# Stick-breaking attention: sums over later key blocks on TensorE instead of GpSimd, float32 scores instead of stacked float32r scores

## The chip, the cores and the metric

The kernel runs on one core of one Trainium2 chip. The metric is the device time of one execution in microseconds (us). The kernel before took 813.81, 815.24 and 815.90 us in three runs; their median, 815.24 us, is "the time before". A core has five engines, named here as in the profile: PE (TensorE, the matrix unit, with PEld for its weight loads), DVE (VectorE), ACT (ScalarE), POOL (GpSimd) and SP (SyncE, which issues DMAs). Matrix products are written to PSUM, which has banks of 512 float32 values per partition; everything else lies in SBUF. Each engine works through its own queue in order.

## The reference, cut to what matters

One decoder layer for 512 tokens of width 1024 in float32: a norm, one wide input projection, two attention branches, a gated merge, an output projection, a SwiGLU feed-forward part and a last norm. The change concerns the first branch, stick-breaking attention with 8 heads of 64 features:

```python
z = einsum('bhqd,bkhd->bhqk', q_blk, k) * scale
causal = kpos[None, :] < tpos[:, None]
log_keep = where(causal, log_sigmoid(-z), 0.0)
log_after = cumsum(log_keep, axis=3, reverse=True) - log_keep
a = where(causal, exp(log_sigmoid(z) + log_after), 0.0)
out = einsum('bhqk,bkhd->bqhd', a, v)
```

With softplus(z) = -log_sigmoid(-z), the log weight of key j for query q is z[j,q] minus the sum of softplus(z[j',q]) over all keys j' from j up to the query. The sum runs over the key's own block of 128 keys and over all later blocks.

## The kernel before, in words

Activations lie feature-major ([feature, token]). Each large product is made of three float32r products, with both operands split into a high and a low part: ACT casts the high part, DVE subtracts to get the low part (`split_to`, lines 103 to 105; weights in `split_chunk`, lines 78 to 85). SP loads the weight chunks of 512 KB. A planner (the tile framework, with a simulated time line) puts the instructions of each engine in a fixed order at build time; instructions whose operands the planner expects in time are interleaved, so the products of later projections stand between those of the attention.

The order of the program is: input and norm; for each of four pairs of heads n the projections of q and k (`proj_feature`, lines 233 to 243; the values v for all heads once, `proj_token`) and then `sb_pair`; the projections of the dilated branch and its attention (`dil_pair`, two pairs); the gates; the merge; the output projection; the feed-forward part, which fills the time from about 400 us on.

PSUM's eight banks are split into 2 for projections ("proj"), 5 for attention ("att") and 1 for outputs ("o") (line 26). SBUF tiles come from pools with a fixed number of buffers (line 27): NT = 10 for the float32 tiles t and r, NR = 9 for the high and low parts h and l, NS = 10 for the stacked operands.

`sb_pair` (lines 297 to 393) handles two heads. Keys are in four blocks a = 0 to 3 of 128; block a has scores for the queries from a x 128 on, thus 512, 384, 256 and 128 columns. Tile names end with the pair's number and with x, y or z: x is a head's blocks 1 and 3 together in one bank (384 + 128 columns), y is block 2 of both heads in one bank (2 x 256), z is a head's block 0 (512). So a pair has five banks: two x, one y, two z.

1. Stacking (lines 302 to 310): for each head ks holds the high and the low part of its 64 key rows above each other on 128 partitions, qa the high part of the queries twice, qb the low part twice. ACT makes three casts, DVE three subtractions per head, on 64 rows x 512.
2. Scores (lines 312 to 325): for blocks 0 to 2 two float32r products over 128 rows (ks with qa, ks with qb); for block 3 one float32 product over the head's 64 rows. A bf16 product of an identity and a mask adds a large negative value where a key isn't before its query.
3. Softplus (`breaks`, lines 327 to 337): ACT takes absolute value, exponent and logarithm, DVE adds max(z, 0), `split_to` makes h and l, and two float32r products with the triangular matrix `tri` (minus one) subtract the block's own running sums in PSUM.
4. Sums for the other blocks (`total`, lines 339 to 342): POOL sums each t tile over the partitions and leaves the sum on all of them (r), three times per pair. POOL adds the sums of several blocks up (lines 364 and 367).
5. Exponents: `later` (lines 346 to 348) subtracts r from PSUM on DVE in the columns that have later key blocks, then ACT takes the exponent; `plain` (lines 350 to 352) takes the exponent directly from PSUM elsewhere.
6. The output product (line 385): float32, the weights of both heads in the two halves of the array's columns, blocks 0 to 3, then a split of the result.

The next pair's score products need the banks that the exponents and subtractions of the pair before give free. In `dil_pair` the score products (lines 398 and 402) are float32 over the 64 rows of one head, 128 columns each.

Of the kernel before, what the change touches and what calls it, by code (L numbers as in the profile page):

```python
# [10 lines left out]
F32 = mybir.dt.float32  # L11
# [15 lines left out]
RAW, NT, NR, NQ, NS = 3, 10, 9, 16, 10  # L27
# [3 lines left out]
def trunk_kernel(ctx, tc, xT, gains, w_in, w_up, w_o, w_f, w_d, bias, out):  # L31
    """Activations are kept feature-major ([feature, token]); the weights are the
    stationary operands. Every float32 operand of the large products is split into
    two float32r parts (hi + lo, exact) and three of the four part products are
    accumulated; the fourth lies below float32's rounding.  The norms' row factors
    commute with the products and are applied where the products leave PSUM."""
# [11 lines left out]
    # products on zeros while the first loads are under way: the PE clock is up when they arrive  # L48
# [127 lines left out]
    V.tensor_copy(tri, tri0)  # L176
    mask0 = ap_.tile([P, S], F32, tag="t", name="mask0", bufs=NT)[:, :2 * P].rearrange("p (a b) -> p a b", a=2)
# [5 lines left out]
    # token blocks of a group: 128 neighbours, or every fourth token (dilation 4; for dilation 16  # L183
    # each such block holds four of the sixteen residues)
# [60 lines left out]
    def proj_token(name, kind, wide):  # L245
        # token-major: the tokens' blocks are stationary, the weights move
        v = ap_.tile([P, 4, wide], F32, tag=name, name=name)
        nk = 1024 // wide
        if wide == 512:
            banks = [bank("att", f"pv{name}{c}") for c in range(4)]  # L250
            order = [(j, c) for j in range(KD // nk) for c in range(4)]
            w = {}
        else:
            w = {0: next_weights(), 1: next_weights(1)}
            order = [(j, c) for c in range(4) for j in range(KD // nk)]
            banks = {}
        for j, c in order:
            if j not in w:
                w[j] = next_weights()
            if c not in banks if wide != 512 else False:  # L260
                banks[c] = bank("proj", f"pv{name}{c}")
            ps = banks[c][:, :wide]
            whi, wlo = w[j]
            for i in range(nk):
                k = j * nk + i
                cs = slice(i * wide, (i + 1) * wide)
                mm3(ps, blk(xh[k], kind, c), blk(xl[k], kind, c), whi[:, cs], wlo[:, cs], k == 0, k == KD - 1)
            if j == KD // nk - 1:
# [26 lines left out]
    # log weight of key j for query q: z[j,q] - sum_{j'>=j} softplus(z[j',q]); key blocks 1 and 3  # L295
    # of a head share a bank, and so do the two heads' blocks 2
    def sb_pair(n, q, k, v, hb):
        hs = [slice(0, 64), slice(64, 128)]

        # both parts of a head's keys fill the 128 rows, so two products carry all four part products  # L300
        ks, qa, qb = [], [], []
        for h in range(2):
            ks.append(stack(f"ks{n}{h}"))
            qa.append(stack(f"qa{n}{h}"))
            qb.append(stack(f"qb{n}{h}"))
            A.copy(ks[h][hs[0]], k[hs[h]])
            V.tensor_tensor(out=ks[h][hs[1]], in0=k[hs[h]], in1=ks[h][hs[0]].bitcast(F32), op=ALU.subtract)
            for r in hs:
                A.copy(qa[h][r], q[hs[h]])
                V.tensor_tensor(out=qb[h][r], in0=q[hs[h]], in1=qa[h][r].bitcast(F32), op=ALU.subtract)  # L310

        def score(ps, o, h, a, start):
            ps = ps[:, o:o + S - a * P]
            if a < 3:
                T.matmul(ps, ks[h][:, a * P:(a + 1) * P], qa[h][:, a * P:], start=start, stop=False, skip_group_check=True)
                T.matmul(ps, ks[h][:, a * P:(a + 1) * P], qb[h][:, a * P:], start=False, stop=False, skip_group_check=True)
            else:
                T.matmul(ps, k[hs[h], a * P:], q[hs[h], a * P:], start=start, stop=False, skip_group_check=True)

        def scores(name, parts, masked):  # L320
            ps = bank("att", f"z{n}{name}")
            for i, (h, a, o) in enumerate(parts):
                score(ps, o, h, a, i == 0)
            T.matmul(ps.rearrange("p (a b) -> p a b", b=P)[:, masked, :], idb, mask[:, :len(parts)], start=False, stop=False, skip_group_check=True)
            return ps

        def breaks(name, ps):
            t = tt(f"t{n}{name}")
# [4 lines left out]
            hi, lo = rt(f"h{n}{name}"), rt(f"l{n}{name}")  # L333
            split_to(hi, lo, t)
            T.matmul(ps, tri, hi, start=False, stop=False, skip_group_check=True)
            T.matmul(ps, tri, lo, start=False, stop=True, skip_group_check=True)
            return ps, t

        def total(name, t):
            r = tt(f"r{n}{name}")  # L340
            G.partition_all_reduce(r, t, P, bass_isa.ReduceOp.add)
            return r

        # A key block's softplus sums count for all the earlier key blocks of the same queries:
        # t = exp(ps - r) in the columns that have later key blocks, exp(ps) in the others
        def later(ps, t, cs, r):
            V.tensor_tensor(out=t[:, cs], in0=ps[:, cs], in1=r, op=ALU.subtract)
            A.activation(t[:, cs], t[:, cs], AF.Exp)

        def plain(ps, t, cols):  # L350
            v = lambda y: y.rearrange("p (a b) -> p a b", b=P)[:, cols, :]
            A.activation(v(t), v(ps), AF.Exp)

        z13 = [scores(f"x{h}", [(h, 1, 0), (h, 3, 384)], slice(0, 4, 3)) for h in range(2)]
        z2 = scores("y", [(0, 2, 0), (1, 2, 256)], slice(0, 4, 2))
        b13 = [breaks(f"x{h}", z13[h]) for h in range(2)]
        b2 = breaks("y", z2)
        r13 = [total(f"x{h}", b13[h][1]) for h in range(2)]
        r2 = total("y", b2[1])
        plain(*b2, slice(0, 4, 2))  # L360
        for h in range(2):
            o = 256 * h
            later(*b2, slice(o + 128, o + 256), r13[h][:, 384:512])
            G.tensor_tensor(out=r2[:, o + 128:o + 256], in0=r2[:, o + 128:o + 256], in1=r13[h][:, 384:512], op=ALU.add)
            plain(*b13[h], slice(0, 4, 3))
            later(*b13[h], slice(128, 384), r2[:, o:o + 256])
            G.tensor_tensor(out=r13[h][:, 128:384], in0=r13[h][:, 128:384], in1=r2[:, o:o + 256], op=ALU.add)
        z0 = [scores(f"z{h}", [(h, 0, 0)], slice(0, 1)) for h in range(2)]
        b0 = [breaks(f"z{h}", z0[h]) for h in range(2)]
        for h in range(2):  # L370
            plain(*b0[h], slice(0, 1))
            later(*b0[h], slice(128, 512), r13[h][:, 0:384])
        po = bank("o", f"o{n}")
        for a in range(4):
            for h in range(2):
                if a == 0:
                    m = b0[h][1]
                elif a == 1:
                    m = b13[h][1][:, 0:384]
                elif a == 2:  # L380
                    m = b2[1][:, 256 * h:256 * h + 256]
                else:
                    m = b13[h][1][:, 384:512]
                c = (hb + h) * 64
                T.matmul(po[hs[h], a * P:], v[:, a, c:c + 64], m, start=a == 0, stop=a == 3, skip_group_check=True)
        split_out(f"s{n}", po)

# [204 lines left out]
    for half in range(2):  # L592
# [5 lines left out]
        if half:  # L598
            # the PE keeps its clock while the norm's row factors are worked out
# [92 lines left out]
```

## Time and profile before

| | |
|---|---|
| median of three timed runs | 815.24 us (813.81 to 815.90) |
| profiled execution, first to last instruction | 814.5 us |
| PE busy | 795.1 us, 98% of the span |
| DVE, ACT, POOL busy | 398.7, 307.7, 123.2 us |
| 51 to 154 us (most of stick-breaking): PE, DVE, ACT, POOL busy of 103.0 | 94.39, 79.13, 75.56, 49.72 |
| PE's mean granted clock, whole span | 0.973 |

All times in the profile are of that one execution; 814.5 us is its span, and what the timed runs have beside it is the 0.7 us by which their median is longer. A row of a timeline has the start, the length, the engine, the line, the operation, the tiles (out<-in), shapes, and in brackets the idle time before it and who ended it. The length of a PE row includes the time in which the next product is already under way, so the cost of a product is read from the distance of two starts. A float32 product leaves two records, a float32r product one. L99, L100 and L101 are the three part products of `mm3`.

### The profile page before, as it was taken

The page shows a single profiled execution, that of the slowest core. Times are in us where ns is not written, and L with a number is a line of the kernel's source. Part 1 is how long each engine was busy: PE and PEld are TensorE (multiplying, and loading weights), DVE is VectorE, ACT ScalarE, POOL GpSimd, SP SyncE. Part 2 cuts the span into 40 slices and gives each one's busy share as a digit, 9 for nine tenths or more (in the row PEclk, how much of TensorE's full clock was granted, in tenths as well). Part 3 has the DMA queues.
Part 4 walks back from the last instruction along what each step waited for, and adds up shares of the span by engine and source line. Part 5 has one row for each costly group of instructions (what it writes and reads, how often), then busy time and mean ns, then how long its engine had stood idle before and what let it go on. Part 6 is the DMA issues. An engine that isn't in the chain of part 4 may idle for free.

```text
span 814.5 us, 9164 instructions
## 1 busy us (share of the span) xinstructions
PE 795.1 (98%) x3635; PEld 649.5 (80%) x3635; DVE 398.7 (49%) x490; ACT 307.7 (38%) x453; POOL 123.2 (15%) x94
## 2 busy tenths in 40 slices
PE   8999988999999999999999999999999999999995
PEld 5877656878997787788888888888888888888885
DVE  6379885543245375438653544444444444322312
ACT  7277865622113335223343432233323322332321
POOL 3424534500003103100232000000000000010012
PEclk9999998999978899999999999999999999999998
DMA  7321111052311103123543223222332333333302
GB/s 234 128 79 52 52 53 52 27 170 89 103 52 52 52 26 105 49 75 109 171 142 102 81 100 104 103 85 97 103 100 83 103 97 97 94 94 97 97 20 103
DMA packets 23786, 74.00 MB, mean 91 GB/s; under 512 B 2608, under 2 KB 5696, under 8 KB 23616
## 3 DMA queue, kind: packets, MB, share of 16 engines
q1 hardware_dynamic: 22928, 70.26, 26.6%
q0 software_dynamic: 816, 3.16, 1.1%
q8 instruction: 28, 0.46, 0.2%
q14 instruction: 14, 0.11, 0.0%
HBM read 71.32 MB, written 2.10 MB: 90 GB/s over the span
## 4 chain that ended last, share of the span: by engine, by line
PE 59%; DVE 0%; ACT 0%; POOL 0%; DVEq 0%; issue 0%; POOLq 0%
PE pd L100 5%; PE pd L101 5%; PE pd L99 5%; PE pu L101 5%; PE pg L101 5%; PE pg L99 5%; PE pu L99 5%; PE pu L100 5%; PE pg L100 5%; PE po L100 2%; PE po L99 2%; PE po L101 2%; PE us L101 1%; PE us L100 1%; PE us L99 1%; PE pjgd L100 1%
## 5 line engine op out<-in xcount | busy, mean ns | idle before, releaser
L83 ACT CAST whi<-raw 128x1024 fp32r<-128x1024 f32 (+1 forms) x128 | 131.2, 1025 | 383.6 <-PE pu L100 77.8
L84 DVE TENSOR_TENSOR wlo<-raw,whi 128x1024 fp32r<-128x1024 f32 (+1 forms) x128 | 159.5, 1247 | 101.8 <-ACT whi L83 101.7
L99 PE MATMUL pd<-hh,whi 128*128 128x512 f32 (+1 forms) x198 | 72.6, 367 | 0.0
L100 PE MATMUL pd<-hl,whi 128*128 128x512 f32 (+1 forms) x198 | 72.4, 366 | 0.0
L101 PE MATMUL pd<-hh,wlo 128*128 128x512 f32 (+1 forms) x198 | 72.3, 365 | 0.0
L101 PE MATMUL pg<-uh,wlo 128*128 128x512 f32 x176 | 68.9, 391 | 0.0
L101 PE MATMUL pu<-uh,wlo 128*128 128x512 f32 x176 | 68.6, 390 | 0.0
L100 PE MATMUL pu<-ul,whi 128*128 128x512 f32 x176 | 68.5, 389 | 0.0
L100 PE MATMUL pg<-ul,whi 128*128 128x512 f32 x176 | 68.5, 389 | 0.0
L99 PE MATMUL pg<-uh,whi 128*128 128x512 f32 x176 | 68.5, 389 | 0.0
L99 PE MATMUL pu<-uh,whi 128*128 128x512 f32 x176 | 68.5, 389 | 0.0
L563 POOL TENSOR_TENSOR acc<-acc,sq 128x512 f32<-128x512 f32 x6 | 7.8, 1298 | 330.0 <-issue 261.6
L541 DVE TENSOR_TENSOR fb<-pu,rb 128x512 f32<-128x512 f32 x22 | 15.2, 691 | 66.8 <-PE pu L101 66.8
L100 PEld LDWEIGHTS pd<-hl,whi 128*128 128x128 f32 x198 | 37.3, 189 | 6.1
L99 PEld LDWEIGHTS pd<-hh,whi 128*128 128x128 f32 x198 | 37.3, 188 | 6.1
L101 PEld LDWEIGHTS pd<-hh,wlo 128*128 128x128 f32 x198 | 37.3, 188 | 5.9
L99 PEld LDWEIGHTS pg<-uh,whi 128*128 128x128 f32 x176 | 33.1, 188 | 7.0 <-issue 0.2
L101 PEld LDWEIGHTS pg<-uh,wlo 128*128 128x128 f32 x176 | 33.0, 187 | 7.1 <-issue 0.2
L100 PEld LDWEIGHTS pu<-ul,whi 128*128 128x128 f32 x176 | 33.0, 188 | 7.0
L101 PEld LDWEIGHTS pu<-uh,wlo 128*128 128x128 f32 x176 | 33.1, 188 | 6.9
L100 PEld LDWEIGHTS pg<-ul,whi 128*128 128x128 f32 x176 | 33.0, 188 | 6.9
L99 PEld LDWEIGHTS pu<-uh,whi 128*128 128x128 f32 x176 | 33.0, 187 | 6.7
(448 smaller groups left out, 1619.8 us busy)
## 6 DMA issues: line engine op xcount, KB each, us to landing
raw<-in_w_in_dram SPq DMA_DIRECT2D x44, 512.0 KB, 3.3
raw<-in_w_ffn_in_dram SPq DMA_DIRECT2D x44, 512.0 KB, 3.3
raw<-in_w_ffn_out_dram SPq DMA_DIRECT2D x16, 512.0 KB, 3.5
raw<-in_w_out_dram SPq DMA_DIRECT2D x8, 512.0 KB, 3.3
raw<-in_w_up_dram SPq DMA_DIRECT2D x8, 384.0 KB, 3.1
raw<-in_w_ffn_out_dram SPq DMA_DIRECT2D x8, 384.0 KB, 3.1
x<-in_xT_dram SPq DMA_DIRECT2D x8, 256.0 KB, 4.7
xall<-in_xT_dram POOLq DMA_DIRECT2D x8, 256.0 KB, 4.7
```

What stands on the lines that cost most here:

```text
L83: A.copy(hi[:, :n], r[:, :n])
L84: V.tensor_tensor(out=lo[:, :n], in0=r[:, :n], in1=hi[:, :n].bitcast(F32), op=ALU.subtract)
L99: T.matmul(ps, shi, mhi, start=first, stop=False)
L100: T.matmul(ps, shi, mlo, start=False, stop=False)
L101: T.matmul(ps, slo, mhi, start=False, stop=last)
L541: V.tensor_tensor(out=b, in0=pu, in1=rb2, op=ALU.mult)
L563: G.tensor_tensor(out=acc3, in0=acc3, in1=sq, op=ALU.add)
```

## The change

`sb_pair` is written anew and a constant `less` (a 128 x 128 matrix of minus one, float32r) is added. The stacking of keys and queries is gone: all scores are float32 products over the 64 rows of a head, head 0 on rows 0 to 63 and head 1 on rows 64 to 127, written in turns. y has a bank for each head. The sums over later blocks are products of `less` with the h and l parts of those blocks, added to the bank in PSUM; POOL has no part in it, and DVE no longer subtracts. The exponent is taken of a whole bank at once. The output product goes over blocks 3, 2, 1, 0. The pools change to NT = 12, NR = 12, NS = 4. Nothing outside is changed but comments.

```diff
-RAW, NT, NR, NQ, NS = 3, 10, 9, 16, 10
+RAW, NT, NR, NQ, NS = 3, 12, 12, 16, 4
...
+    less = cp.tile([P, P], F32R)
+    V.tensor_scalar_mul(less, ones, -1.0)
...
-        ks, qa, qb = [], [], []
-        for h in range(2):
...
-            A.copy(ks[h][hs[0]], k[hs[h]])
-            V.tensor_tensor(out=ks[h][hs[1]], in0=k[hs[h]], in1=ks[h][hs[0]].bitcast(F32), op=ALU.subtract)
-            for r in hs:
-                A.copy(qa[h][r], q[hs[h]])
-                V.tensor_tensor(out=qb[h][r], in0=q[hs[h]], in1=qa[h][r].bitcast(F32), op=ALU.subtract)
...
+        def scores(name, blocks):
+            ps = [bank("att", f"z{name}{n}{h}") for h in range(2)]
+            o = 0
+            for i, a in enumerate(blocks):
+                for h in range(2):
+                    T.matmul(ps[h][:, o:o + S - a * P], k[hs[h], a * P:(a + 1) * P], q[hs[h], a * P:], start=i == 0, stop=False, skip_group_check=True)
+                o += S - a * P
+            for h in range(2):
+                cols = slice(0, 4, 3) if len(blocks) > 1 else slice(0, 1)
+                T.matmul(ps[h].rearrange("p (a b) -> p a b", b=P)[:, cols, :], idb, mask[:, :len(blocks)], start=False, stop=False, skip_group_check=True)
+            return [p[:, :o] for p in ps]
...
-        def total(name, t):
-            r = tt(f"r{n}{name}")
-            G.partition_all_reduce(r, t, P, bass_isa.ReduceOp.add)
-            return r
...
+        def take(ps, w, parts, cs, last=False):
+            for i, t in enumerate(parts):
+                T.matmul(ps, w, t[:, cs], start=False, stop=last and i == 1, skip_group_check=True)
+
+        own = slice(None)
+        zx = scores("x", (1, 3))
+        zy = scores("y", (2,))
+        bx = [breaks(f"x{h}", zx[h]) for h in range(2)]
+        by = [breaks(f"y{h}", zy[h]) for h in range(2)]
         for h in range(2):
...
+            take(zy[h], tri, by[h][1], own)
+            take(zy[h][:, 128:256], less, bx[h][1], slice(384, 512), True)
+            A.activation(by[h][0], zy[h], AF.Exp)
+            take(zx[h], tri, bx[h][1], own)
+            take(zx[h][:, 256:384], less, bx[h][1], slice(384, 512))
+            take(zx[h][:, 128:384], less, by[h][1], own, True)
+            A.activation(bx[h][0], zx[h], AF.Exp)
+        zz = scores("z", (0,))
+        bz = [breaks(f"z{h}", zz[h]) for h in range(2)]
         for h in range(2):
...
+            take(zz[h], tri, bz[h][1], own)
+            take(zz[h][:, 128:512], less, bx[h][1], slice(0, 384))
+            take(zz[h][:, 256:512], less, by[h][1], own)
+            take(zz[h][:, 384:512], less, bx[h][1], slice(384, 512), True)
+            A.activation(bz[h][0], zz[h], AF.Exp)
         po = bank("o", f"o{n}")
-        for a in range(4):
+        for a in (3, 2, 1, 0):
```

More of the change, by code (lines that the diff above doesn't have):

```diff
@@ L298, in sb_pair @@
         hs = [slice(0, 64), slice(64, 128)]
-        ks, qa, qb = [], [], []
-        for h in range(2):
-            ks.append(stack(f"ks{n}{h}"))
-            qa.append(stack(f"qa{n}{h}"))
-            qb.append(stack(f"qb{n}{h}"))
-            A.copy(ks[h][hs[0]], k[hs[h]])
-            V.tensor_tensor(out=ks[h][hs[1]], in0=k[hs[h]], in1=ks[h][hs[0]].bitcast(F32), op=ALU.subtract)
-            for r in hs:
[L309 to L325, printed above, removed]
+        def scores(name, blocks):
[9 more added lines that the diff above has]
+            return [p[:, :o] for p in ps]
         def breaks(name, ps):
-            t = tt(f"t{n}{name}")
+            w = ps.shape[-1]
+            t = tt(f"t{n}{name}")[:, :w]
             A.activation(t, ps, AF.Abs)
@@ L332, in breaks @@
             V.scalar_tensor_tensor(out=t, in0=ps, scalar=0.0, in1=t, op0=ALU.max, op1=ALU.add)
-            hi, lo = rt(f"h{n}{name}"), rt(f"l{n}{name}")
+            hi, lo = rt(f"h{n}{name}")[:, :w], rt(f"l{n}{name}")[:, :w]
             split_to(hi, lo, t)
-            T.matmul(ps, tri, hi, start=False, stop=False, skip_group_check=True)
-            T.matmul(ps, tri, lo, start=False, stop=True, skip_group_check=True)
-            return ps, t
-        def total(name, t):
-            r = tt(f"r{n}{name}")
-            G.partition_all_reduce(r, t, P, bass_isa.ReduceOp.add)
-            return r
@@ L346, in later @@
[L346 to L360, printed above, removed]
-        for h in range(2):
[L362 to L367, printed above, removed]
@@ L368, in sb_pair @@
-        z0 = [scores(f"z{h}", [(h, 0, 0)], slice(0, 1)) for h in range(2)]
-        b0 = [breaks(f"z{h}", z0[h]) for h in range(2)]
-        for h in range(2):
-            plain(*b0[h], slice(0, 1))
-            later(*b0[h], slice(128, 512), r13[h][:, 0:384])
+            return t, (hi, lo)
+        def take(ps, w, parts, cs, last=False):
+            for i, t in enumerate(parts):
+                T.matmul(ps, w, t[:, cs], start=False, stop=last and i == 1, skip_group_check=True)
+        own = slice(None)
@@ L375, in sb_pair @@
             for h in range(2):
                 if a == 0:
-                    m = b0[h][1]
+                    m = bz[h][0]
                 elif a == 1:
-                    m = b13[h][1][:, 0:384]
+                    m = bx[h][0][:, 0:384]
                 elif a == 2:
-                    m = b2[1][:, 256 * h:256 * h + 256]
+                    m = by[h][0]
                 else:
-                    m = b13[h][1][:, 384:512]
+                    m = bx[h][0][:, 384:512]
                 c = (hb + h) * 64
-                T.matmul(po[hs[h], a * P:], v[:, a, c:c + 64], m, start=a == 0, stop=a == 3, skip_group_check=True)
+                T.matmul(po[hs[h], a * P:], v[:, a, c:c + 64], m, start=a == 3, stop=a == 0, skip_group_check=True)
```

## The prediction

> **What bounds the kernel now.** I read the page first, then stretches of the span, then the matmul engine's waits, then the timelines around those waits.
>
> ```profile
> span 814.5 us, 9164 instructions
> PE 795.1 (98%) x3635; PEld 649.5 (80%) x3635; DVE 398.7 (49%) x490; ACT 307.7 (38%) x453; POOL 123.2 (15%) x94
> ```
>
> TensorE (PE) has work 98% of the time, so a microsecond of PE work added anywhere is a microsecond of time, unless it replaces idle time or time at a low clock. The next view gives the stick-breaking stretch and the long feed-forward stretch (columns: stretch, length, busy time and count of PE, its weight loads, DVE, ACT, POOL, then granted clock, DMA share, GB/s).
>
> ```profile
> 51.00:154.00 103.00, 94.39 (x440) 69.67 (x439) 79.13 (x99) 75.56 (x147) 49.72 (x24) 0.95 0.17 57
> 300.00:800.00 500.00, 499.74 (x2290) 413.64 (x2289) 223.33 (x267) 162.65 (x204) 36.68 (x30) 1.00 0.29 94
> ```
>
> In 300 to 800 PE idles 0.26 us: there is nothing to win there and the change doesn't touch it. In 51 to 154 PE idles 103.00 - 94.39 = 8.6 us. The waits of PE say for whom:
>
> ```profile
> PE z3x L315 <- DVE t2x L347: 3.3, 1, 3.3
> PE z2x L315 <- DVE t1x L347: 2.7, 1, 2.7
> PE z1x L336 <- DVE l1x L105: 2.0, 1, 2.0
> PE z1x L315 <- DVE t0x L347: 0.6, 2, 0.4
> ```
>
> 3.3 + 2.7 + 2.0 + 0.6 = 8.6, so these four rows are the whole idle time. Three are the next pair's first score product, waiting for a PSUM bank whose last reader is the subtraction of L347. The timelines of POOL and DVE show what that one was late for:
>
> ```profile
> 93.07 3.46 POOL L341 PARTITION_ALL_REDUCE r1y<-t1y  x1
> 103.55 0.86 POOL L364 TENSOR_TENSOR r1y<-r1y,r1x 128x128 f32<-128x128 f32 x2 [7.02 <-issue]
> 135.58 0.86 POOL L364 TENSOR_TENSOR r2y<-r2y,r2x 128x128 f32<-128x128 f32 x2 [7.09 <-issue]
> ```
> ```profile
> 93.47 2.62 DVE L105 TENSOR_TENSOR l1x<-t1x,h1x 128x512 fp32r<-128x512 f32 x1
> 96.01 0.68 DVE L105 TENSOR_TENSOR l1y<-t1y,h1y 128x512 fp32r<-128x512 f32 x1
> 104.03 0.42 DVE L347 TENSOR_TENSOR t1x<-z1x,r1y 128x256 f32<-128x256 f32 x1 [4.35 <-POOL r1y L364]
> ```
>
> POOL ends the last sum over partitions at 96.5 and starts the add only at 103.55: 7.02 us in which it waits for nothing visible, and 7.09 in the next pair. DVE and then PE wait behind it. The 2.0 us wait is POOL's too: the same DVE instruction takes 2.62 us while a partition sum runs and 0.68 us just after. Two of the waits also cost clock:
>
> ```profile
> 104.60:108.00 3.40, 3.40 (x10) 2.54 (x11) 3.34 (x3) 1.96 (x3) 2.18 (x2) 0.57 0.20 73
> 135.30:142.10 6.80, 5.48 (x16) 3.29 (x16) 4.08 (x8) 5.06 (x13) 2.23 (x4) 0.54 0.00 0
> ```
>
> Right behind the gaps PE works 3.40 us at a clock of 0.57 and 5.48 us at 0.54; at full clock that would take 3.40 x 0.43 + 5.48 x 0.46 = 4.0 us less. So POOL's detour costs PE 8.6 + 4.0 = **12.6 us**.
>
> The Trainium skill ("TensorE: Matmul & The Clock Gate", its table of goals at the end) sees the danger for PE gaps beyond about 3 us. Here the clock had fallen after one of 2.67 us; by the page only the 3.3 us gap would have done it, and 1.5 us less would come back.
>
> **The change part by part.** *POOL's sums and the subtractions of L347 go.* With them go the 7 us detour, the slowed DVE instructions and the whole 12.6 us, if nothing new is late. I keep 1.5 us back for new waits: after the change a pair asks for six banks (x, y, z of both heads) where the pool has five, so the second z waits until a y or x bank has had its exponent. Ends: 0 and 12.6 us, the latter if the gaps stay as they are.
>
> *The casts (ACT) and subtractions (DVE) that stack keys and queries go too*, three of each per head:
>
> ```profile
> L309 ACT CAST qa<-sq 64x512 fp32r<-64x512 f32 x13 | 8.0, 618 | 0.2
> L310 DVE TENSOR_TENSOR qb<-sq,qa 64x512 fp32r<-64x512 f32 x14 | 10.9, 781 | 1.3 <-ACT qa L309 0.8
> ```
>
> Six of each in a pair are 3.7 us of ACT and 4.7 us of DVE. PE is the bound, so I give this no price of its own; it makes it likelier that the scores' operands and exponents are in time. The extra constant (one small DVE copy in the first 50 us), the tile counts and y's steps in two halves cost ACT and DVE a little and PE nothing, as long as their load per pair stays under PE's. A bias load on POOL's queue, which waited for the fourth pair's output product, can only start earlier.
>
> *The sums come back as PE products* with the stationary "less": per head 12 float32r products, six 128 columns wide (2 for y, 2 for x, 2 for z), four of 256, two of 384. Prices by distance between starts:
>
> ```profile
> 79.29 0.28 PE L316 MATMUL z1y<-qb,ks 128*128 128x256 f32 x1
> 79.41 0.27 PE L315 MATMUL z1y<-qa,ks 128*128 128x256 f32 x1
> ...
> 145.87 0.48 PE L315 MATMUL z3z<-qa,ks 128*128 128x512 f32 x1
> 146.19 0.40 PE L316 MATMUL z3z<-qb,ks 128*128 128x512 f32 x1
> 146.43 0.23 PE L324 MATMUL z3z<-mask,idb 128*128 128x128 bf16 x1
> 146.47 0.36 PE L99 MATMUL pvvd<-whi,xh 128*128 128x256 f32 x1
> 146.67 0.28 PE L100 MATMUL pvvd<-wlo,xh 128*128 128x256 f32 x1
> ```
>
> 256 columns take 0.12 us, 512 take 0.24, so 384 take 0.18 by proportion. No float32r product of 128 columns is in the trace. The nearest is the mask: from 146.43 to 146.67 a mask of 128 columns and a product of 256 take 0.24, so the mask takes 0.24 - 0.12 = 0.12, no less than 256 columns. I take 0.12. Lower end: a quarter of 512, 0.06. Upper end, a float32r product that falls to float32's rate; that rate is in these rows:
>
> ```profile
> 41.88 1.02 PE L211 MATMUL rb<-dg,ones 128*128 128x512 f32 x2
> 42.33 0.79 PE L99 MATMUL pvvs<-whi,xh 128*128 128x512 f32 x1
> 42.97 0.40 PE L100 MATMUL pvvs<-wlo,xh 128*128 128x512 f32 x1
> ```
>
> One float32 product of 512 columns (two records) and one float32r take 42.97 - 41.88 = 1.09, so float32 takes 0.86, and 128 columns 0.215. Per head: 6 x 0.12 + 4 x 0.12 + 2 x 0.18 = 1.56 us; eight heads **+12.5 us** (ends 8 x 1.20 = 9.6 and 8 x 2.13 = 17.0).
>
> *The scores.* Before, one head's x (with mask) and one head's z take:
>
> ```profile
> 74.69 0.41 PE L315 MATMUL z1x<-qa,ks 128*128 128x384 f32 x1 [0.18 <-DVE t0x L347]
> ...
> 75.66 0.47 PE L335 MATMUL z0z<-h0z,tri 128*128 128x512 f32 x1
> ...
> 85.00 0.39 PE L315 MATMUL z1z<-qa,ks 128*128 128x512 f32 x1
> ...
> 85.50 0.48 PE L315 MATMUL z1z<-qa,ks 128*128 128x512 f32 x1
> ```
>
> 0.97 and 0.50; y is four products of 256 and a mask, 0.6. A pair: 2 x 0.97 + 0.6 + 2 x 0.5 = 3.54 us. Of x's 0.97, the two float32r products (0.36), the float32 one (0.215) and the mask (0.12) explain 0.69; the other 0.28 I put down to going into 64 rows and out again. After: 1280 float32 columns per head, 1280 / 512 x 0.86 = 2.15 us. Whether two heads cost that once or twice is in these rows, where products of two heads lie on the two row halves:
>
> ```profile
> 228.65 5.01 PE L398 MATMUL d<-dq,dk 64*128 64x128 f32 x24
> 233.49 0.51 PE L402 MATMUL d<-dq,dk 64*128 64x128 f32 x3
> ...
> 233.95 0.27 PE L398 MATMUL d<-dq,dk 64*128 64x128 f32 x1
> 233.95 0.27 PE L402 MATMUL d<-dq,dk 64*128 64x128 f32 x1
> 234.06 0.27 PE L398 MATMUL d<-dq,dk 64*128 64x128 f32 x1
> 234.06 0.27 PE L402 MATMUL d<-dq,dk 64*128 64x128 f32 x1
> ```
>
> In one half 24 records take 4.84 us, 0.20 each; where the halves alternate, two start together and the next two follow 0.11 us later. So neighbours in the queue do run side by side. Paired, a pair of heads costs 2.15 + six masks 0.72 + three excursions into 64 rows 0.84 = 3.71 us, +0.17 per pair, +0.7 in all. Unpaired it costs 2.15 more, +9.3 in all. They pair only if both heads' banks are free together: likely for x, doubtful for y and z with five banks for six tiles. I let half of y's and z's (256 + 512) / 512 x 0.86 = 1.29 us go unpaired: 0.65 per pair, **+3.3 us** in all.
>
> The Trainium skill (the same page, Part 3, measured speedups) has four row tiles at 3.07 times instead of four. An estimate by it for two halves would be 1.53 times, the paired 2.15 would be 2.8, and the forecast up to 2.6 us later; the rows above show nearly the full factor.
>
> *The output products* run over the blocks in another order. Two heads together take as long as one alone:
>
> ```profile
> 86.96 1.08 PE L385 MATMUL o<-t0z,vs 128*64 128x512 f32 x4
> ...
> 114.11 1.07 PE L385 MATMUL o<-t1z,vs 128*64 128x512 f32 x2
> ```
>
> The first head went alone at 114.11; with z now last this may still happen, so zero (ends -1 us and +1 us a pair).
>
> **Sum.** 814.5 + 12.5 + 3.3 - 12.6 + 1.5 = 819.2 us of span. The timed runs' median, 815.24, lies 0.7 above the profiled span, so **820 us**.
>
> **Rivals.** *Faster: PE runs small products at the streaming price.* The repeated stationary hides the weight loads, a 128-wide product costs 0.06, and the heads pair up: 814.5 + 9.6 + 0.7 - 12.6 - 1.0 (outputs) + 0.7 = 812. For it: neighbours on two halves hide all loads. Against: the mask's 0.12. It decides, with all heads paired and no new wait, from an average "less" product of (12.6 - 0.7) / 96 = 0.124 us down, where I have 12.5 / 96 = 0.130. *No change:* heads pair up, no new wait, 128 columns at 0.12: 814.5 + 12.5 + 0.7 - 12.6 + 0.7 = 816. *128-wide float32r at float32's rate:* +4.5, 824.5; for it, that the kernel gives its 128-wide score block to plain float32; against it, no row. *The banks are the new wait:* PE's queue is in order, so a z score that waits for an exponent holds the projections behind it; 2 us a pair and no clock regained for it, 820 + 6 = 826. *The detour is not what holds PE* (only the order of the queue): nothing comes back, 814.5 + 12.5 + 3.3 + 0.7 = 831; the waits' rows speak against it.
>
> **Chances.** Forecast 0.38 (0.07 of it near enough to no change), faster rival 0.22, no change 0.12 (0.02 of it faster), float32's rate 0.13, banks 0.10, no detour 0.05. A difference of 0.3%, 2.4 us, is about what this kernel's measurement can tell. Faster 0.24, same 0.07 + 0.10 = 0.17, slower 0.59. The range, 810 to 829, takes in the faster rival and the bank case and leaves out the last; the forecast's own is 816.5 to 823.5.
>
> **What would show it.** In 51 to 154 (some microseconds longer): idle PE time down from 8.6 to about 1.5 us, clock near 1.00, no POOL work, every l tile near 0.7 us. The "less" rows: starts 0.12 apart at 128 columns (0.06 and 0.21 are the rivals). Score records of two heads starting together, x surely, y and z in half of the cases. After 300 everything as before. I am wrong if idle time stays above 5 us, or if a stretch that the change doesn't touch moves by more than 2 us.

## The result and the profile after

The changed kernel takes **834.16 us** (median; 832.26 to 834.99) beside 815.57 us (813.81 to 816.53) of the kernel before on the same chip: 1.0228 times as long, 95% interval 1.0210 to 1.0246. The direction was forecast, the size was not: 834.16 lies above the range of 810 to 829. The profiled execution went from 814.5 to 832.2 us. The page of the changed kernel, its first lines:

```profile
span 832.2 us, 9230 instructions
PE 814.7 (98%) x3743; PEld 659.9 (79%) x3743; DVE 359.0 (43%) x451; ACT 294.5 (35%) x425; POOL 70.1 (8%) x66
```

POOL, DVE and ACT have less to do, as meant. PE's busy time grew by 814.7 - 795.1 = 19.6 us, the span by 17.7. The stretches say where (columns as in the prediction). The changed kernel:

```profile
51.00:154.00 103.00, 103.00 (x488) 70.01 (x487) 45.46 (x69) 66.61 (x131) 0.00 (x0) 1.00 0.15 47
45.40:237.60 192.20, 192.20 (x921) 147.44 (x919) 70.68 (x94) 88.24 (x156) 0.61 (x1) 1.00 0.22 72
237.63:382.06 144.43, 137.31 (x633) 111.70 (x633) 67.25 (x81) 44.39 (x57) 23.82 (x16) 0.87 0.16 54
```

The kernel before, for the same work:

```profile
45.40:228.60 183.20, 174.59 (x814) 139.52 (x812) 109.33 (x134) 101.25 (x184) 53.72 (x29) 0.97 0.23 75
228.60:364.30 135.70, 135.44 (x633) 109.63 (x633) 68.56 (x81) 44.30 (x57) 23.75 (x16) 0.91 0.18 58
```

Two stretches of work are compared. The first goes from the second pair's q projection to the first score of the dilated branch ("the stick-breaking stretch"): 183.2 became 192.2 us, +9.0. The second goes from there to the first product of the merge ("the dilated stretch"): 135.7 became 144.4, **+8.75, in code that the diff doesn't touch**. What comes after takes 450.1 us in both.

In the stick-breaking stretch PE now idles not at all (192.20 of 192.20 at a granted clock of 1.00; between 51 and 154 us, too, 103.00 of 103.00). So what POOL cost is all back, and more than that is paid in products. The next table adds up, for this stretch, the distance from each PE record's start to the next one's, by kind of product, less idle time. Work at the low clock is counted at half its time, the rest of it in the last row.

| us in the stick-breaking stretch | before | after | difference |
|---|---|---|---|
| projections | 134.5 | 135.2 | +0.7 |
| scores and masks | 14.3 | 19.8 | +5.5 |
| products with `tri` | 9.9 | 10.8 | +0.9 |
| products with `less` | - | 11.4 | +11.4 |
| output products | 11.2 | 15.0 | +3.8 |
| idle, and extra time at the low clock | 13.3 | 0 | -13.3 |
| sum | 183.2 | 192.2 | +9.0 |

The timeline of PE in the changed kernel, for each of the new costs:

```profile
63.74 0.22 PE L329 MATMUL zx<-h0x,less 128*128 128x128 f32 x1
63.80 0.28 PE L329 MATMUL zx<-l0x,less 128*128 128x128 f32 x1
63.91 0.33 PE L329 MATMUL zy<-h0y,tri 128*128 128x256 f32 x1
...
70.56 1.14 PE L309 MATMUL zx<-sq,sk 64*128 64x384 f32 x8
71.64 0.32 PE L364 MATMUL o<-t0x,vs 128*64 128x128 f32 x1
...
84.90 1.07 PE L364 MATMUL o<-t0z,vs 128*64 128x512 f32 x2
85.90 1.12 PE L309 MATMUL zz<-sq,sk 64*128 64x512 f32 x2
86.96 0.51 PE L329 MATMUL zx<-h1x,tri 128*128 128x512 f32 x1
```

A product of 128 columns with `less` takes 63.80 - 63.74 = 0.06 us here when its twin (the same stationary) follows, and 63.91 - 63.80 = 0.11 up to another stationary; the 48 of the stretch average 0.09. The x scores of both heads together (eight records, 1024 columns) take 71.64 - 70.56 = 1.08, so they run side by side. But a z score of one head, 512 columns, goes alone and takes 86.96 - 85.90 = 1.06, as much as both heads would take together; all eight do. So does the output product of one head's z, 85.90 - 84.90 = 1.00.

In the dilated stretch one wait of PE has grown. `dl` is the product with ones that sums a head's weights over the keys. The row of the kernel before, and that of the changed one:

```profile
PE dl L446 <- POOL m L430: 0.3, 1, 0.3
```
```profile
PE dl L425 <- POOL m L409: 7.1, 1, 7.1
```

POOL's timeline there, of the changed kernel:

```profile
246.67 1.81 POOL L402 PARTITION_ALL_REDUCE mb<-m  x1 [82.61 <-DVE m L400]
258.38 1.78 POOL L402 PARTITION_ALL_REDUCE mb<-m  x1 [9.91 <-issue]
267.12 1.28 POOL L407 TENSOR_TENSOR m<-p,p 128x512 f32<-128x512 f32 x1 [6.95 <-issue]
...
304.07 1.50 POOL L408 TENSOR_TENSOR m<-m,p 128x512 f32<-128x512 f32 x1
311.47 1.80 POOL L402 PARTITION_ALL_REDUCE mb<-m  x1 [5.91 <-PE pjgd L101]
320.97 0.98 POOL L409 TENSOR_TENSOR m<-m,p 128x384 f32<-128x384 f32 x1 [7.70 <-issue]
```

Per head POOL makes one maximum over partitions (L402) and three adds (L407 to L409). Before, the order was maximum, adds, maximum, adds; these rows of the kernel before are the first head's last add and the second head's maximum:

```profile
309.06 1.22 POOL L430 TENSOR_TENSOR m<-m,p 128x384 f32<-128x384 f32 x1
316.23 1.80 POOL L423 PARTITION_ALL_REDUCE mb<-m  x1 [5.95 <-issue]
```

Now the second head's maximum stands ahead of the first head's last add: POOL turns to it at 311.47 after 5.91 us without an instruction in the timeline, turns back after 7.70, and `dl`, which needs that last add, holds PE's queue for 7.1 us. Had POOL gone straight on to it, the add would have been done in time: the add ahead of it ended at 304.07 + 1.50 = 305.57, ACT had made the last exponent that it needs by 302.9, and PE came to `dl` at 322.01 - 7.12 = 314.89. The clock falls too, by the windows of the changed kernel:

```profile
322.00:328.00 6.00, 5.99 (x26) 3.38 (x28) 1.55 (x2) 1.68 (x2) 3.45 (x3) 0.55 0.00 0
```

5.99 us of work at 0.55 are 2.7 us lost. This agrees with the Trainium skill ("TensorE: Matmul & The Clock Gate", its table of goals), which warns of PE gaps beyond about 3 us. Shorter gaps were followed by a low clock here as well: 2.67 us in the kernel before, 2.3 us in experiment 1.

### The profile page after: what moved, and what is told of

The parts are those of the page before. It is cut to its first block, busy times and chain, and to the rows that moved or that the text cites. A ratio compares the mean times of both kernels' runs of the same rounds, so it can differ in the third digit from the quotient of the medians.

```text
span 832.2 us, 9230 instructions
## 1 busy us (share of the span) xinstructions
PE 814.7 (98%) x3743; PEld 659.9 (79%) x3743; DVE 359.0 (43%) x451; ACT 294.5 (35%) x425; POOL 70.1 (8%) x66
## 4 chain that ended last, share of the span: by engine, by line
PE 60%; issue 0%; POOL 0%; DVE 0%; ACT 0%; DVEq 0%; POOLq 0%
PE pd L99 5%; PE pd L101 5%; PE pd L100 5%; PE pu L101 5%; PE pg L99 5%; PE pu L99 5%; PE pu L100 5%; PE pg L100 5%; PE pg L101 5%; PE po L101 2%; PE po L100 2%; PE po L99 2%; PE pjgd L99 1%; PE pjgd L101 1%; PE pjgd L100 1%; PE pjgs L100 1%
```

## The experiments

The theory now: (1) 12 instead of 10 buffers for t tiles, a number in line 27, let the planner write another order for the dilated branch, and POOL's detour makes that order wait; (2) in stick-breaking PE pays for heads whose products don't stand next to each other (z scores, outputs), and for the sums themselves; (3) POOL's detour, not its work, was the gain to be had. The rivals: that the dilated stretch moved because the work ahead of it came later; that the float32 scores, not their pairing, are dear; that POOL's sums over partitions are themselves too slow. Each ratio is to the kernel before, timed on the same chip.

### 1. The buffers alone, in the kernel before

```diff
-RAW, NT, NR, NQ, NS = 3, 10, 9, 16, 10
+RAW, NT, NR, NQ, NS = 3, 12, 9, 16, 9
```

One stacked tile (NS) was given up, for room. A control gives up that tile alone.

```diff
-RAW, NT, NR, NQ, NS = 3, 10, 9, 16, 10
+RAW, NT, NR, NQ, NS = 3, 10, 9, 16, 9
```

> The kernel before with 12 instead of 10 buffers for the float32 tiles (and 9 instead of 10 stacked operands, to fit). Theory 1 (tile count): the stick-breaking attention stays at 183 us from the second pair's q projection to the first dilated score (45.5 to 228.7 in the trace of before), and the stretch from there to the first merge product grows from 135.7 us to 143 to 146, because with 12 buffers the second head's partition maximum goes ahead of the first head's adds in POOL's queue and POOL changes between the two kinds of work once more; in all 822 to 826 us. Rival 2 (the dilated stretch is longer after the change only because it starts later, at another phase of the clock, or because POOL had no partition sums before): 815 to 817 us and 134 to 138 us.

> Control for the kernel before with 12 t tiles, which had to give up one of ten stacked tiles: here only that one is given up (NS = 9, NT stays 10). Theory 1 (the 8 us came from the t tiles): within 1 us of the kernel before, ratio 0.998 to 1.002. Theory 2 (the missing stacked tile made the loss, or part of it): 2 to 8 us slower, ratio 1.003 to 1.010.

Measured: 822.17 us, ratio 1.0097 (1.0066 to 1.0127); the control 815.30 us, 1.0002 (0.9988 to 1.0017). The waits of PE with 12 tiles, in the kernel before:

```profile
PE dl L446 <- POOL m L430: 8.3, 2, 7.0
PE z2x L315 <- DVE t1x L347: 2.3, 1, 2.3
```

The new row is that of the changed kernel, and the dilated stretch takes 143.8 us instead of 135.7. **Two more buffers, with nothing else of the change, cost about 8 us.** That the stretch came later isn't needed for it.

### 2. The changed kernel with 10 tiles

```diff
-RAW, NT, NR, NQ, NS = 3, 12, 12, 16, 4
+RAW, NT, NR, NQ, NS = 3, 10, 12, 16, 4
```

> The changed kernel with 10 instead of 12 buffers for the float32 tiles. Theory 1: the dilated stretch goes back from 144.4 us to 135 to 137, the 7.1 us wait of PE for POOL's add is gone, in all 825 to 827 us; the stick-breaking stretch stays at 192 us. Rival 2: 833 to 835 us.

Measured: 824.28 us, ratio 1.0124 (1.0100 to 1.0148): 9.9 us less than with 12, or 8.5 by the two ratios. Its dilated stretch in the windows:

```profile
237.05:372.00 134.95, 134.75 (x633) 109.41 (x633) 68.54 (x81) 44.19 (x57) 23.78 (x16) 0.91 0.18 58
```

The stick-breaking stretch stays at 192.2 us to a tenth. So the two losses are separate and were cut cleanly in two.

### 3. What in the order of 12 tiles costs the time

First, POOL's order is put back (`G` is POOL, `NOSYNC` an order without a wait); the planner writes the other queues anew around it:

```diff
+    adds = []
...
-            G.partition_all_reduce(mb, m, P, bass_isa.ReduceOp.max)
+            r = G.partition_all_reduce(mb, m, P, bass_isa.ReduceOp.max)
+            if adds:
+                tc.add_manual_dep(r.ins, adds[-1].ins.name, NOSYNC, reason="issue order")
...
-            G.tensor_tensor(out=m[:, P:], in0=m[:, P:], in1=tl[3][:, P:], op=ALU.add)
+            adds.append(G.tensor_tensor(out=m[:, P:], in0=m[:, P:], in1=tl[3][:, P:], op=ALU.add))
```

> The changed kernel with its 12 tiles; only POOL's order in the dilated attention is written out: a head's partition maximum (L402) comes behind the last add of the head before it. Nothing is left out. Theory 1 (the 12 tiles cost time only because they let the maximum go ahead of those adds, so that POOL pays its detour more often): the matmul engine's 7 us waits for the normaliser's sum go, the dilated stretch falls from 144 to about 135 us, and the time is about 825 us (823 to 828), ratio 1.010 to 1.015. Theory 2 (12 tiles cost time by another way, such as the order of DVE or ACT): the stretch stays at 142 or more and the time at 831 to 836.

Measured: 837.49 us, ratio 1.0283 (1.0254 to 1.0312), dilated stretch 145.8. My theory failed: putting POOL's order back doesn't mend the stretch. POOL now goes maximum, adds, maximum, adds, and PE waits all the same, in other places. PE's waits and, below them, the timelines of POOL and PE, of this kernel:

```profile
PE dl L429 <- POOL m L413: 6.4, 2, 4.0
PE n L420 <- ACT p L410: 1.8, 1, 1.8
```
```profile
267.19 1.80 POOL L404 PARTITION_ALL_REDUCE mb<-m  x1 [5.77 <-issue]
276.20 1.26 POOL L411 TENSOR_TENSOR m<-p,p 128x512 f32<-128x512 f32 x1 [7.20 <-issue]
277.54 1.26 POOL L412 TENSOR_TENSOR m<-m,p 128x512 f32<-128x512 f32 x1
278.88 0.99 POOL L413 TENSOR_TENSOR m<-m,p 128x384 f32<-128x384 f32 x1
```
```profile
276.76 0.82 PE L379 MATMUL d<-dq,dk 64*128 64x128 f32 x2
279.93 1.51 PE L429 MATMUL dl<-m,ones 128*64 128x512 f32 x2 [2.34 <-POOL m L413]
```

Between the `dl` of the first pair's two heads PE's queue has only attention products here (22 records of scores, and the products `n` of weights and values); with 10 tiles, as in the kernel before, 30 projection products stand there too. They take 9.0 us in experiment 2, where PE comes to the second `dl` at 287.97, over 4 us behind the end of the last add. So PE's queue is tight here although POOL's order is the old one. But it isn't the queue of the changed kernel: there the `dl` products of the first pair's two heads follow each other from 276.71 on and wait for nothing. This run shows that POOL's old order alone is no remedy; it doesn't clear POOL's order of the 7.1 us in the changed kernel.

Second, the 12 tiles stay and POOL's changes of work are taken away: DVE makes the three adds.

```diff
-            G.tensor_tensor(out=m, in0=tl[0], in1=tl[1], op=ALU.add)
-            G.tensor_tensor(out=m, in0=m, in1=tl[2], op=ALU.add)
-            G.tensor_tensor(out=m[:, P:], in0=m[:, P:], in1=tl[3][:, P:], op=ALU.add)
+            V.tensor_tensor(out=m, in0=tl[0], in1=tl[1], op=ALU.add)
+            V.tensor_tensor(out=m, in0=m, in1=tl[2], op=ALU.add)
+            V.tensor_tensor(out=m[:, P:], in0=m[:, P:], in1=tl[3][:, P:], op=ALU.add)
```

> The changed kernel with its 12 tiles; the three adds of a head's weights in the dilated attention (L407 to L409) are made by DVE, so POOL has only the four partition maxima there and changes its kind of work no more. Nothing is left out; the queue of the matmul engine stays nearly as it was in this stretch. Theory 1 (the waits of the 12-tile order are made by POOL's 6 to 8 us between a maximum and an add): the matmul engine's wait for the normaliser's sum goes or is under 1 us, the dilated stretch takes 133 to 138 us where it took 144.4, and the time is 823 to 828. Theory 2 (the order of 12 tiles is too tight whoever adds: the sums are late because of the exponents before them): some 4 to 8 us of waits stay and the time is 830 to 836.

Measured: 825.96 us, ratio 1.0125 (1.0110 to 1.0141), the same as with 10 tiles. The windows of the dilated stretch and POOL's timeline, of this kernel:

```profile
237.93:373.69 135.76, 135.76 (x633) 110.64 (x633) 71.90 (x93) 44.19 (x57) 7.15 (x4) 0.91 0.18 58
```
```profile
246.85 1.80 POOL L402 PARTITION_ALL_REDUCE mb<-m  x1 [82.49 <-DVE m L400]
257.78 1.78 POOL L402 PARTITION_ALL_REDUCE mb<-m  x1 [9.13 <-issue]
```

The second maximum still goes ahead, the two `dl` of a pair still stand close (at 268.65 and 275.74 in the first), and PE idles no more. So the 8.75 us are the order of 12 tiles *and* POOL's detour together; 10 tiles bring them back, and so does DVE in POOL's place. PE's order differs between all these kernels, so how much each turn of the order costs can't be told.

### 4. The two heads' output products next to each other

On top of 10 tiles, the eight output products of a pair are held in the queue until the second head's z exponent (an order, no wait of their own):

```diff
-            A.activation(bz[h][0], zz[h], AF.Exp)
+            behind = A.activation(bz[h][0], zz[h], AF.Exp)
...
-                T.matmul(po[hs[h], a * P:], v[:, a, c:c + 64], m, start=a == 3, stop=a == 0, skip_group_check=True)
+                om = T.matmul(po[hs[h], a * P:], v[:, a, c:c + 64], m, start=a == 3, stop=a == 0, skip_group_check=True)
+                tc.add_manual_dep(om.ins, behind.ins.name, NOSYNC, reason="issue order")
```

> The changed kernel with 10 buffers, and the eight output products of a pair of heads held in the queue until the second head's z exponent, so that the two heads' products stand side by side. Theory 3 (pairing): the output products cost 15.0 us in the changed kernel against 11.0 before because the last z product of each head runs alone; side by side they cost 9 to 10 us, the stick-breaking stretch is 186 to 188 us, in all 819 to 821 us. Rival 4 (they cost more for another reason, such as changes between array shapes, or holding them back makes PE wait): 15 us still, 825 to 830 us.

Measured: 819.61 us, ratio 1.0055 (1.0034 to 1.0076), 4.7 less than before the edit. PE's timeline of it:

```profile
86.09 0.44 PE L364 MATMUL o<-t0x,vs 128*64 128x128 f32 x4
86.36 0.60 PE L364 MATMUL o<-t0y,vs 128*64 128x256 f32 x4
86.79 0.81 PE L364 MATMUL o<-t0x,vs 128*64 128x384 f32 x4
87.44 1.03 PE L364 MATMUL o<-t0z,vs 128*64 128x512 f32 x4
88.39 0.38 PE L329 MATMUL zy<-l1y,tri 128*128 128x256 f32 x1
```

Two heads' z products now take 88.39 - 87.44 = 0.95, where one alone took 1.00. Outputs fell from 15.0 to 9.2 us, `tri` by 0.6, scores rose by 0.8; the stretch went from 192.2 to 186.5. The dilated stretch took 2.2 more (134.95 to 137.1), 1.7 of it extra time at the low clock.

### 5. The scores of both heads next to each other

Six attention banks instead of five, and the z scores held until the first head's y exponent, so that both heads' banks are free. The sixth bank is that of the outputs. In a first version the two early norms use the joined pool as well.

```diff
-BANKS = {"proj": 2, "att": 5, "o": 1}
+BANKS = {"proj": 2, "att": 6}
...
     def bank(tag, name):
+        tag = "att" if tag == "o" else tag
...
-        zz = scores("z", (0,))
+        zz = scores("z", (0,), zafter)
```

> The last one with six instead of five attention banks (the output's bank joins them), and the z scores of both heads held until both banks are free, so that all scores of two heads stand side by side in the queue. Theory 3: scores fall from 17.3 us to 11 to 13, outputs to 9 to 10, the stick-breaking stretch to 181 to 184 us, in all 813 to 817 us. Rival 4 (pairing is worth little, or the longer chain of a pair of heads brings waits of PE): 819 us or more, with idle PE time in the stick-breaking stretch.

Measured: 832.88 us, ratio 1.0224 (1.0193 to 1.0255), a miss. PE's waits of it:

```profile
PE ss L197 <- POOL acc L127: 13.9, 2, 10.0
PE rb L214 <- ACT dg L210: 6.4, 3, 2.7
```

Neither row has to do with attention: the products `ss` and `rb` of the norms, with a bank of the joined pool at hand, were put earlier in PE's queue than their operands come. In the stick-breaking stretch itself PE doesn't idle. So a second version opens the pool of six only after the values' projection, behind the first norm, and gives the later norm's products a projection bank:

```diff
...
             vs = proj_token("vs", 0, 512)
+            six_banks()
```

> The full pairing once more: changed kernel, 10 buffers, outputs of two heads side by side, six attention banks and all scores of two heads side by side; but the banks are made six only after the values' projection, so that the first norm's products keep their place in the queue (in the run before they were put ahead and PE waited 9.95 us for the input's sums of squares). Theory 3 (pairing): scores plus masks 10 to 13 us against 19.7 in the changed kernel, stick-breaking stretch 175 to 178 us, in all 807 to 812 us, which is less than before. Rival 4: 817 us or more, with waits of PE in the stick-breaking stretch.

Measured: **807.82 us**, ratio 0.9922 (0.9892 to 0.9952). The changed kernel's way of computing is faster than the kernel before, once 10 tiles, the outputs and the scores are in order: its stick-breaking stretch takes 177.7 us against 183.2 before. PE's timeline and the windows of this kernel:

```profile
66.34 1.13 PE L322 MATMUL zz<-sq,sk 64*128 64x512 f32 x4
67.40 0.28 PE L328 MATMUL zz<-mask,idb 128*128 128x128 bf16 x2
```
```profile
43.87:221.60 177.73, 177.73 (x921) 144.57 (x919) 69.50 (x94) 86.58 (x156) 0.61 (x1) 1.00 0.23 78
```

Both heads' z scores take 67.40 - 66.34 = 1.06, the time of one alone in the changed kernel. Scores fell from 18.2 to 11.1 us over the stretch, which went from 186.5 to 177.7. The dilated stretch gave 4.1 more (137.1 to 133.0), 3.4 of it less time at the low clock; no run here tells why, so about a third of what this version gained isn't shown to be the pairing's.

### 6. Stacked float32r scores in place of float32

The changed kernel with 10 tiles, and in it the stacking (lines 302 to 310 of before, with NS = 8) and the two float32r products per block; the sums stay on PE.

```diff
...
-                    T.matmul(ps[h][:, o:o + S - a * P], k[hs[h], a * P:(a + 1) * P], q[hs[h], a * P:], start=i == 0, stop=False, skip_group_check=True)
...
+                T.matmul(ps, ks[h][:, a * P:(a + 1) * P], qa[h][:, a * P:], start=start, stop=False, skip_group_check=True)
+                T.matmul(ps, ks[h][:, a * P:(a + 1) * P], qb[h][:, a * P:], start=False, stop=False, skip_group_check=True)
```

> The changed kernel with 10 buffers and one part undone: the scores are again float32r products of stacked keys and queries; the sums stay on PE. Theory 5 (sums and scores each cost what the accounts say): scores and masks 14 to 15 us instead of 19.7, the sums 11.4 us as they are, no wait of PE; the stick-breaking stretch 186 to 188 us, in all 818 to 821 us. Rival: with the casts and subtractions back, ACT and DVE are too late again and PE waits 3 us or more: 822 to 826 us.

Measured: 818.69 us, ratio 1.0053 (1.0033 to 1.0073), 5.6 less than with float32 scores. Scores and masks take 15.1 us instead of 19.8, so **float32 scores that pair only in part are dearer than stacked ones, and all paired (13.1 us in experiment 5) they are cheaper**. The rival, that float32 as such is the loss, falls.

### 7. The kernel before, with DVE making POOL's adds

The sums over partitions stay on POOL; only the adds of L364 and L367, four per pair, move.

```diff
-            G.tensor_tensor(out=r2[:, o + 128:o + 256], in0=r2[:, o + 128:o + 256], in1=r13[h][:, 384:512], op=ALU.add)
+            V.tensor_tensor(out=r2[:, o + 128:o + 256], in0=r2[:, o + 128:o + 256], in1=r13[h][:, 384:512], op=ALU.add)
...
-            G.tensor_tensor(out=r13[h][:, 128:384], in0=r13[h][:, 128:384], in1=r2[:, o:o + 256], op=ALU.add)
+            V.tensor_tensor(out=r13[h][:, 128:384], in0=r13[h][:, 128:384], in1=r2[:, o:o + 256], op=ALU.add)
```

> The kernel before with one edit: the four adds per pair that follow the partition sums go from POOL to DVE, so that POOL does partition sums alone. Theory 6 (POOL's 7 us between a partition sum and an add is what PE waits for): of 8.6 us idle 2 stay (the slow DVE subtraction during a partition sum), the low clock in this stretch goes, stick-breaking stretch 173 to 176 us, in all 803 to 807 us. Rival 7 (the partition sums themselves, or the order of the queue, hold PE): 811 to 816 us.

Measured: **804.07 us** (802.59 to 805.29), ratio 0.9877 (0.9850 to 0.9905): the fastest version here, beside the one below, with two letters changed. Its timelines of POOL and DVE, its waits of PE and its windows:

```profile
84.95 4.06 POOL L341 PARTITION_ALL_REDUCE r1x<-t1x  x1 [0.33 <-DVE t1x L332]
88.91 3.46 POOL L341 PARTITION_ALL_REDUCE r1y<-t1y  x1
```
```profile
95.75 0.48 DVE L364 TENSOR_TENSOR r1y<-r1y,r1x 128x128 f32<-128x128 f32 x2
96.98 0.42 DVE L347 TENSOR_TENSOR t1x<-z1x,r1y 128x256 f32<-128x256 f32 x1
```
```profile
PE z1y L336 <- DVE l1y L105: 0.6, 1, 0.6
```
```profile
43.28:215.90 172.62, 172.04 (x813) 138.25 (x811) 113.32 (x150) 100.51 (x184) 41.32 (x13) 1.00 0.24 80
```

The sum ends at 92.4, DVE adds at 95.75 and subtracts at 96.98; before, the same subtraction came 7.5 us behind the end of the sum (104.03 and 96.5), here 4.6. Of 8.6 us of waits 0.6 are left, and the clock stays at 1.00. POOL's sums over partitions cost PE next to nothing; the change from them to an ordinary add did.

Two variants of it. In one the output products are held as in experiment 4:

> The last one with a pair's output products held until the second head's z exponents, so that more of them stand side by side. Theory 3: outputs fall from 11.0 to 9 to 10 us, 1 to 2 us less in all than without. Rival 4: no gain, or PE waits for the held products and it is slower.

Measured: 805.34 us, ratio 0.9887 (0.9863 to 0.9910). Outputs fell only from 13.2 to 12.2 us, since not all of them came together, and the dilated stretch took 2.6 more: no gain that can be told, a miss. In the other the adds of the dilated branch are DVE's as well:

> The kernel before with the four adds of each stick-breaking pair and the three adds of each dilated head on DVE: POOL has only sums and maxima over partitions. Nothing is left out. The waits of the matmul engine in the dilated stretch were only 0.3 us before, but 12 us went there to a low granted clock. Theory 1 (the low clock there is not POOL's): the time is that of the kernel with the four adds alone on DVE, 802 to 806. Theory 2 (the clock falls because products are held by POOL's sums, only with other products in between): 3 to 8 us less, 796 to 801.

Measured: 804.06 us, ratio 0.9848 (0.9829 to 0.9867), the same time within the intervals. With 10 tiles the dilated order has room for POOL's detour, so taking it away there gives nothing that can be told.

## Why the prediction was right and wrong

The forecast's span was 819.2 us; it came out at 832.2. The 13.0 us between them, by the steps of the prediction:

| step, as the prediction put it | forecast | shown | adds |
|---|---|---|---|
| "the tile counts ... cost ... PE nothing" | 0 | 8.75 | +8.75 |
| output products: "so zero (ends -1 us and +1 us a pair)" | 0 | 3.8 | +3.8 |
| scores and masks: half of y's and z's unpaired | 3.3 | 5.5 | +2.2 |
| y's steps in two halves, the rest of the stretch | 0 | 1.6 | +1.6 |
| "less" products | 12.5 | 11.4 | -1.1 |
| POOL's waits and clock | -12.6 | -13.3 | -0.7 |
| new waits kept back | 1.5 | 0 | -1.5 |

**The step that failed** is the one that priced the tile counts at nothing. I had asked only whether ACT and DVE can carry the load, not what the planner does with more buffers in a stretch whose code isn't changed. "After 300 everything as before" was wrong for the same reason: the waits there were 0.3 us because POOL took the heads one by one and PE had projection products to cover its detour, and with two more buffers the planner wrote an order that the detour no longer fits. In the changed kernel it put the second head's maximum ahead of the add that `dl` waits for. Experiments 1 and 2 show the size, 3 shows that the detour is needed for it. That putting POOL's own order back would mend it, my first theory, is refuted; the share of that order in the changed kernel's 7.1 us is not.

**Right in kind, wrong in size.** The output products, I had said, may still go alone; those of z all did, and the total came out near the upper end that I had given (4 x 1 us). Scores pair where they stand together, as the dilated rows had shown. But for z I let half pair and none did: a z score of one head takes 1.06 us, eight 8.4, while four pairs take 4.2 in experiment 5. y paired by half and x mostly.

**Right.** POOL's detour was what PE waited for, and all of it came back; the rival that the order alone holds PE is out, by experiment 7 as well. The banks became no wait: PE doesn't idle, the planner paid with scores taken one by one instead. The sums were priced a tenth too high: products of 128 columns average 0.09 us, midway between my 0.12 and the faster rival's 0.06. That rival had the right pairing of heads in mind, but needed an order that the planner didn't give; experiment 5, which gives it, comes to 807.82.

**Left over.** The median stands 2.0 us above the profiled span, where it stood 0.7 above it before: 1.3 us of the 14.2 by which the forecast's 820 was passed, which the profile can't place.

## What to carry to other kernels

A buffer count is part of the schedule: before pricing a change at its own lines, run the old kernel with the new counts alone, here one line and 8 us. Products that share the array by halves cost the same alone as in a pair, so a gain from pairing has to be written into the queue's order, and its buffers must be free for both at once. When an engine stands between two waits, look first at what it does between its instructions: moving four small adds per pair off POOL gave more than rewriting the attention to do without it.

## What the runs showed of the hardware beyond that

- **POOL's change of work.** Between a sum or maximum over partitions and an ordinary add POOL spends 5.77 to 7.70 us in the rows above, in both directions, without an instruction in the timelines. Asked by line, the trace of the kernel before has one more kind of row for the adds of L364:

```profile
L364 POOLq MODIFY_POOL_CONFIG  x8: 87/88/88, 66.5 to 153.7; - x8
```

  That is a pair of instructions of POOL's sequencer for each of the four changes to an add; ahead of the add that starts at 103.55 they stand at 96.48 and 96.51, where the sum ends. From 40 to 345 us such a pair stands at every change, in both directions, and nowhere else; in the first kernel of experiment 7, whose stick-breaking adds are DVE's, there is none between 35 and 226 us. The Trainium skill ("GPSIMD Engine Reference", Instruction dispatch) has about 6 us, without a visible instruction, for the first call to freshly loaded code. The size agrees, and the pairs fit it; what they load at each change is not shown by a run here.
- **The clock falls while PE is busy.** In the dilated stretch of the kernel before, of the changed one and of those of experiments 5 and 7 (last variant), a low clock begins 3.4 to 6.1 us behind the start of each run of 24 or more records of dilated scores (64 rows, 128 columns; three such runs in each kernel). Windows of the kernel before:

```profile
240.00:246.00 6.00, 6.00 (x21) 5.21 (x21) 3.04 (x6) 0.63 (x1) 0.00 (x0) 0.50 0.00 0
```

  PE is busy for 6.00 of 6.00 us at a clock of 0.50 and no idle time stands ahead of it in this stretch; without any of POOL's detours (experiment 7's last variant) it stays. It costs 10 to 14 us in the dilated stretch of the versions in which PE hardly waits there. That the products on half of the rows set it off is only argued, and such products don't stand ahead of every fall: in the kernel before the clock also fell at 33.38, with PE busy, for 3.41 us, behind sixteen records of products over all rows but one column wide (30.46 to 33.13).
